# Block zero's v, r, q and k as seven half products, its weight pieces stored at once, a reordered end and one branch around two loops

## The chip, the cores and the metric

The kernel runs on one core of one Trainium2 chip. The metric is the device time of one launch in microseconds (us), the median of three runs.

## The reference, cut to what matters

A decoder block over 2048 tokens of width 1024. A projection makes q, k, v, r, a low-rank decay input, a pooling input u and two gates; the mixers' outputs are merged and projected; a router sends each token to two of 32 experts; a last norm ends it.

```python
h = rmsnorm(x, norm1_g)
q, k, v, r, a_low, u_pool, gate_gla, gate_pool = split(h @ w_in)
log_a = log_sigmoid(a_low @ w_alpha_up + b_alpha) / 16
o = head_rmsnorm(gla_mix(q, k, v, log_a), gla_norm_g) * silu(r)
y_gla  = o @ w_gla_branch
y_pool = pool_mix(u_pool, pool_w, pool_scale) @ w_pool_branch
x = x + (sigmoid(gate_gla) * y_gla + sigmoid(gate_pool) * y_pool) @ w_out
x = x + hier_moe(rmsnorm(x, norm2_g), ...)        # top-2 of 32 SwiGLU experts
return rmsnorm(x, norm_f_g)
```

## The kernel before

The mixer works on four blocks of 512 tokens (blocks 0 to 3, `block`, L802), the experts follow in 16 pairs (`moe`, L1131). Every projection is done in three passes of float16 halves: a float32 weight piece of 128x1024 is loaded on SyncE's queue (`stage`, L159), split into a high and a low half by one ScalarE instruction (L177) and one VectorE instruction (L178), and multiplied by the high and low halves of the activations. A split piece can be stored in HBM (L181, also on SyncE's queue) and only loaded in the later blocks (L170). `KEEP` (L193) says from which block on each kind of weight is stored: q, k, u (kind 0), v and r (kind 1), the output weight (kind 3) and the gla branch (kind 4) from block 1, gates and pool branch from block 0. So block 1 loads and splits again what block 0 has split. Float32 pieces and split pieces share one pool of 13 buffers (`NW`, L204).

Two projections that share their input (v with r, gate with gate, q with k, u with u) are done together in seven half-size products instead of eight, of weight pieces and differences of weight pieces (`less`, L395, on GpSimd, L398) with the activations `hT` and with sums and differences of the activations `hS` (`p0_norm`'s `sums`, L287; turned by DMA on SyncE's queue, `turn`, L261). The products are put together on VectorE (L348 for the 512 wide ones, L527 for those of q, k and u, 256 wide). `seven` (L323) takes the products in the order A11, S1, S3, S4, S2, A12, A22; S1 to S4 need `hS`, the A ones only `hT`.

Block 0 is different. Its v is done in whole products as soon as a token tile is turned (`p3v`, L594, called from `hybrid`, L1461), its r likewise (`p3r`, L600), and its q and k in whole products (`WHOLE`, L552, `whole` in `seven_c`, L508). The decay (`p1a`, `p1b`, `p1c`) stands between v and q.

At the end, each expert pair's three row groups are added up (`D`: L1322, L1334), normed, scaled and scattered to HBM (`F`: `finish`, L1339, `scatter`, L1283). Then come two loops over counts held in a table (`overflow`, L1374), which run zero times for these inputs. The order of instructions on each engine is set when the program is built, by a list scheduler.

Of the kernel before, what the change touches and what calls it, by code (L numbers as in the profile page):

```python
# [17 lines left out]
KT = 8  # L18
# [18 lines left out]
class Mixer:  # L37
# [51 lines left out]
    def consts2(self):  # L89
# [22 lines left out]
        self.g2q = self.cx.tile([128, D], F32, name="g2q")  # L112
        V.tensor_scalar(self.g2q, self.g2, float(D) ** 0.5, None, op0=OP.mult)
# [79 lines left out]
    KEEP = (1, 1, 0, 1, 1, 0)  # L193
# [22 lines left out]
    def normed(self, x, g, store=None, quick=False, new=None):  # L216

        nc = self.nc
        if quick:
# [11 lines left out]
            for y, n in zip(ys, q):  # L231
                nc.vector.scalar_tensor_tensor(y, x[:, n], r[:, 0:1], self.g2q[:, n], op0=OP.mult, op1=OP.mult)
# [319 lines left out]
    WHOLE = (1, 0)  # L552
# [54 lines left out]
    def p3(self, fill):  # L607
# [11 lines left out]
        self.seven(self.L7, V0, R0, self.et, post, fill)  # L619
# [182 lines left out]
    def block(self, b, tail):  # L802
# [60 lines left out]
        if last:  # L863
            self.xo = {t: self.x_load(b, t) for t in range(TT)}
# [206 lines left out]
    def spill(self):  # L1071
# [31 lines left out]
        V.tensor_scalar(none[:, 0:1], none[:, 0:1], 0.5, None, op0=OP.is_lt)  # L1103
        for _, _, l, _ in self.tab:
# [26 lines left out]
    def moe(self):  # L1131
# [18 lines left out]
        with tc.manual_schedule(engines={getattr(E, e) for e in self.MANUAL}) if self.MANUAL else ExitStack():  # L1150
            for P in range(self.NP + 1):
                for c in (self.PLAN if P else self.PLAN.replace("U0 A0 U1 A1", "V0 V1 W0 A0 W1 A1")).split():
# [186 lines left out]
    def finish(self, s, i):  # L1339

        nc = self.nc
        x, o, _, l, nl = s["X"][i]
        y, r = self.rstd(x)
# [7 lines left out]
        nc.vector.tensor_tensor(y, x, y, op=OP.mult)  # L1351
        t = self.scatter(y, o).ins
# [21 lines left out]
    def overflow(self):  # L1374
# [7 lines left out]
        with tc.For_i(0, n):  # L1382
            T = lambda name, sh, dt=F32: mp.tile([128] + sh, dt, name="o" + name)
            le = T("le", [32])
            V.tensor_scalar(le, self.ct, self.it, None, op0=OP.is_le)
            e = T("e", [1])
            V.tensor_reduce(e, le, axis=AX.X, op=OP.add)
            ei = T("ei", [1], I32)
            V.tensor_copy(ei, e)
            V.tensor_scalar(le, self.i32, e, None, op0=OP.is_equal)  # L1390
            st = T("st", [32])
            V.tensor_tensor(st, self.ct, self.nt, op=OP.subtract)
            V.tensor_tensor(st, st, le, op=OP.mult)
            base = T("base", [1])
            V.tensor_reduce(base, st, axis=AX.X, op=OP.add)
            V.tensor_tensor(base, self.it, base, op=OP.subtract)
            V.tensor_tensor(st, self.capE, le, op=OP.mult)
            cap = T("capt", [1])
            V.tensor_reduce(cap, st, axis=AX.X, op=OP.add)
            V.scalar_tensor_tensor(base, base, 128.0, cap, op0=OP.mult, op1=OP.add)  # L1400
            rel, oth = T("rel", [nt * 2]), T("oth", [nt * 2])
            V.tensor_scalar(oth, self.ex.rearrange("p t k -> p (t k)"), e, OOB, op0=OP.not_equal, op1=OP.mult)
            V.tensor_scalar(rel, self.rk.rearrange("p t k -> p (t k)"), base, None, op0=OP.subtract)
            V.tensor_tensor(rel, rel, oth, op=OP.add)
            io = T("io", [128])
            nc.gpsimd.iota(io, pattern=[[1, 128]], base=0, channel_multiplier=0, allow_small_or_imprecise_dtypes=True)
            pt = self.aux()
            for c in range(2 * nt):
                a = mp.tile([128, 128], F32, name="oA", bufs=1)
                V.tensor_scalar(a, io, rel[:, c:c + 1], None, op0=OP.is_equal)  # L1410
                nc.tensor.matmul(pt[:, 0:2], a, self.fld[:, c // 2, c % 2], start=c == 0, stop=c == 2 * nt - 1)
            tb = T("tb", [2, 1])
            V.tensor_copy(tb, pt[:, 0:2, None])
            ii, w, _, _ = self.columns(tb, "o", mp)
            er = nc.values_load(ei[0:1, 0:1], engines=[mybir.EngineType.SP], min_val=0, max_val=NE - 1,
# [32 lines left out]
def hybrid(tc, A, out, NTOK=2048, cap=CAP, dbg=None):  # L1448
    nc = tc.nc
    with ExitStack() as ctx:  # L1450
# [82 lines left out]
```

## Time and profile before

| | |
|---|---|
| time, median of 3 runs | 1668.42 us (1664.65 to 1674.61) |
| profiled execution: its own time | 1676.06 us |
| its span | 1674.3 us |
| mean granted TensorE clock | 0.96 |
| TensorE busy | 1530.3 us, 91% |
| VectorE busy | 1074.3 us, 64% |
| ScalarE / GpSimd busy | 686.0 us / 607.7 us |
| mean rate of the DMA engines | 236 GB/s |

A share is that of the whole span. The blocks lie at 0 to 336.5 us (block 0), to 627.7 us (block 1), to 898.4 us (block 2) and to about 1169 us (block 3); a block is counted from its first v or r matmul (in blocks 1 to 3, L339) to that of the next. The expert pairs follow.

### The profile page before, as it was taken

To read this page: it belongs to the slowest core of one execution; us is meant where nothing else is said; L and a number is where in the kernel's file an instruction comes from. 1 tells how busy PE (TensorE), PEld (TensorE's weight loads), DVE (VectorE), ACT (ScalarE), POOL (GpSimd) and SP (SyncE) were. 2 spreads that over 40 slices of the span, in tenths; PEclk is the share of its full clock that TensorE was granted. 3 is DMA by queue.
4 is the path that set the end of the run, shared out by engine and by line. 5 is a ranking of instruction groups with operands and counts; after the bars stand their busy time and mean duration, and the time that the engine had idled before them with its cause. 6 is when DMAs were issued, how large, how long until landed. Compare 5 with 4: busy or idle time off the path is not lost.

```text
span 1674.3 us, 27694 instructions
## 1 busy us (share of the span) xinstructions
PE 1530.3 (91%) x10587; PEld 914.6 (55%) x10587; DVE 1074.3 (64%) x1898; ACT 686.0 (41%) x1056; POOL 607.7 (36%) x543
## 2 busy tenths in 40 slices
PE   5898978987999898999989999996799999999994
PEld 3364333435744343764434674443668787777773
DVE  8669685589954543772624674337577777777762
ACT  5623453453223352122423021113356665666661
POOL 1356382356523401342322241121343444444431
PEclk9999999989999999999989999998799999999997
DMA  7434659797775989565878756759599999999941
GB/s 267 133 117 141 232 189 249 230 293 234 231 259 164 250 287 286 182 194 179 231 192 246 245 160 201 204 159 315 187 313 332 336 328 341 333 325 326 330 164 43
DMA packets 244808, 394.65 MB, mean 236 GB/s; under 512 B 154507, under 2 KB 157963, under 8 KB 244672
## 3 DMA queue, kind: packets, MB, share of 16 engines
q1 hardware_dynamic: 222144, 324.50, 62.5%
q0 software_dynamic: 22528, 68.35, 11.5%
q8 instruction: 84, 1.38, 0.3%
q14 instruction: 52, 0.43, 0.1%
HBM read 294.03 MB, written 75.50 MB: 221 GB/s over the span
## 4 chain that ended last, share of the span: by engine, by line
PE 66%; DVE 11%; DMA 7%; issue 6%; POOL 4%; SPq 3%; ACT 2%; POOLq 0%; DVEq 0%; ACTq 0%
PE acc L1297 14%; PE aux L339 8%; PE acc L774 8%; PE acc L339 8%; PE acc L1322 7%; PE acc L522 6%; PE acc L757 6%; DMA w<-in_wv_dram 4%; PE acc L1334 3%; DVE w L178 3%; DMA bt<-bt 2%; SPq L261 2%; PE auxh L1241 2%; PE acc L591 1%; POOL w L398 1%
## 5 line engine op out<-in xcount | busy, mean ns | idle before, releaser
L1297 PE MATMUL acc<-xT,mwh 128*128 128x184 f16 (+2 forms) x3264 | 249.8, 239 | 0.0
L1297 PEld LDWEIGHTS <-mwh 128*128 128x128 f16 x3264 | 244.6, 98 | 7.6 <-issue 7.6
L178 DVE SCALAR_TENSOR_TENSOR w<-w 128x1024 f16<-128x1024 f32 x106 | 144.2, 1369 | 88.5 <-ACT w L177 88.2
L774 PE MATMUL acc<-w,bt 128*128 128x512 f16 x768 | 174.4, 389 | 16.1 <-DMA bt<-bt 12.9
L339 PEld LDWEIGHTS <-hS 128*128 128x128 f16 x1056 | 104.5, 100 | 133.4 <-issue 18.0
L757 PE MATMUL acc<-w,bt 128*128 128x512 f16 x768 | 169.0, 381 | 7.1 <-ACT w L177 7.1
L177 ACT ACTIVATE w<-w 128x1024 f16<-128x1024 f32 x106 | 108.0, 1028 | 151.8 <-DMA w<-in_wv_dram 75.2
L1203 DVE SCALAR_TENSOR_TENSOR mwh<-mst,mwh 128x1024 f16<-128x1024 f32 x128 | 153.4, 1219 | 23.6 <-ACT mwh L1202 23.4
L1202 ACT ACTIVATE mwh<-mst 128x1024 f16<-128x1024 f32 x128 | 128.7, 1049 | 60.7 <-PE acc L1297 59.8
L774 PEld LDWEIGHTS <-bt 128*128 128x128 f16 x768 | 76.0, 100 | 113.2 <-issue 14.5
L339 PE MATMUL aux<-w,hS 128*128 128x512 f16 x528 | 131.6, 398 | 4.5 <-DVE w L178 2.5
L339 PEld LDWEIGHTS <-hT 128*128 128x128 f16 x792 | 77.2, 98 | 100.9 <-issue 11.1
L522 PEld LDWEIGHTS <-w 128*128 128x128 f16 x1176 | 114.3, 100 | 32.4 <-issue 10.5
L757 PEld LDWEIGHTS <-bt 128*128 128x128 f16 x768 | 75.3, 98 | 99.9 <-issue 10.9
L339 PE MATMUL acc<-w,hS 128*128 128x512 f16 x528 | 123.1, 382 | 0.0
L1322 PE MATMUL acc<-msd,sg 128*128 128x512 f32 x256 | 115.7, 605 | 0.0
L762 POOL TENSOR_TENSOR et<-et 128x512 f32<-128x512 f32 x32 | 40.5, 1269 | 174.9 <-DVE et L760 174.9
L684 ACT ACTIVATE bt<-et 128x512 f16<-128x512 f32 x48 | 30.2, 628 | 174.4 <-POOL et L762 100.6
L348 DVE SCALAR_TENSOR_TENSOR et<-aux,et 128x512 f32<-128x512 f32 x99 | 65.8, 683 | 53.5 <-PE aux L339 53.5
L339 PE MATMUL aux<-w,hT 128*128 128x512 f16 x396 | 91.8, 379 | 5.7 <-DVE w L178 3.3
L760 DVE SCALAR_TENSOR_TENSOR et<-acc,et 128x512 f32<-128x512 f32 x64 | 43.3, 689 | 82.4 <-PE acc L757 82.4
L339 PE MATMUL acc<-w,hT 128*128 128x512 f16 x396 | 92.3, 379 | 0.9 <-DVE w L178 0.9
(293 smaller groups left out, 2493.8 us busy)
## 6 DMA issues: line engine op xcount, KB each, us to landing
w<-wkeep SPq DMA_DIRECT2D x172, 512.0 KB, 4.7
mst<-in_we_dram SPq DMA_DIRECT2D x128, 512.0 KB, 6.0
wkeep<-w SPq DMA_DIRECT2D x70, 512.0 KB, 3.3
msd<-in_we_dram SPq DMA_DIRECT2D x64, 512.0 KB, 7.1
w<-in_wv_dram SPq DMA_DIRECT2D x60, 512.0 KB, 4.9
x<-in_x_dram SPq DMA_DIRECT2D x32, 512.0 KB, 5.5
w<-in_wm_dram SPq DMA_DIRECT2D x16, 512.0 KB, 6.1
out_dram<-x POOLq DMA_DIRECT2D x16, 512.0 KB, 5.8
```

The lines of the kernel that those rows point to most:

```text
L177: nc.scalar.activation(w[:, 0, c:], f[:, c:], AF.Copy, scale=WSC)
L178: nc.vector.scalar_tensor_tensor(w[:, 1, c:], f[:, c:], WSC, w[:, 0, c:], op0=OP.mult, op1=OP.subtract)
L339: nc.tensor.matmul(p, L[name](i, c, k), w[k // 2][:, a, (k % 2) * 512:(k % 2 + 1) * 512], start=k == 0 and m == 0, stop=k == 3 and m == 2)
L348: nc.vector.scalar_tensor_tensor(o[i], ps[i], DSC, x[i], op0=OP.mult, op1=OP.add)
L522: nc.tensor.matmul(ps[:, :h], w[:, i, k * 128:(k + 1) * 128], L[name](c, k), start=k == 0 and m == 0, stop=k == 3 and m == 2)
L757: nc.tensor.matmul(ps, lhs, w[k // 2][:, a, (k % 2) * 512:(k % 2 + 1) * 512], start=k == 0 and i == 0, stop=k == 3 and i == 2)
L774: nc.tensor.matmul(ps, self.mT[t][k // 4][:, 4 * c + k % 4], w[hf][k // 2][:, a, (k % 2) * 512:(k % 2 + 1) * 512], start=k == 0 and i == 0 ...
L1202: nc.scalar.activation(w[:, 0], f, AF.Copy, scale=WSC)
L1203: nc.vector.scalar_tensor_tensor(w[:, 1], f, WSC, w[:, 0], op0=OP.mult, op1=OP.subtract)
L1297: nc.tensor.matmul(ps[:, c * CAP + lo:c * CAP + hi], self.part(W[o], col, 128, a), xT[:, b, k, lo:hi], start=k == 0 and i == 0, stop=k == ...
L1322: nc.tensor.matmul(ps, s["ac"][i][:, f, :128], self.part(s["W"][3 * i + 2], f * D + hf * 512, 512), start=f == 0, stop=f == 1)
L1334: nc.tensor.matmul(ps[hf * 64:(hf + 1) * 64], s["ac"][h][:, f, CAP - 64:], self.part(s["W"][3 * h + 2], f * D + hf * 512, 512), start=q == ...
```

## The change

Block 0's v and r are done in seven half products too, as are its q and k (`WHOLE` is zero); all split pieces are stored from block 0 on (`KEEP` is zero). v and r get a product loop and a weight order of their own in every block, the two products that need no sums first. In block 0 all four tiles are normed and turned before the sums are formed, and the decay steps lie between the products. A scaled copy of the second norm's gain is dropped; the gain is scaled in place in block 3. The last two expert pairs norm by another sequence of instructions, the last pair does its third row group first, and one branch stands around both loops at the end (their bodies are unchanged, one level deeper).

```diff
-        self.g2q = self.cx.tile([128, D], F32, name="g2q")
-        V.tensor_scalar(self.g2q, self.g2, float(D) ** 0.5, None, op0=OP.mult)
...
-    KEEP = (1, 1, 0, 1, 1, 0)
+    KEEP = (0, 0, 0, 0, 0, 0)
...
-    def p0_turn(self, i, hh, dma=True):
-        if i == 0:
+    def p0_turn(self, i, hh, dma=True, parts=(0, 1)):
+        if i == 0 and 0 in parts:
...
-        for j, t in enumerate((i, i + 2)):
-            self.turn(hh[j], lambda a: H[:, a, :, t * 128:(t + 1) * 128], dma)
-        for j in range(2):
-            self.turn(hh[2 + j], lambda a: HS[:, i, j, a], True)
+        if 0 in parts:
+            for j, t in enumerate((i, i + 2)):
+                self.turn(hh[j], lambda a: H[:, a, :, t * 128:(t + 1) * 128], dma)
+        if 1 in parts:
+            for j in range(2):
+                self.turn(hh[2 + j], lambda a: HS[:, i, j, a], True)
...
-    WHOLE = (1, 0)
+    WHOLE = (0, 0)
...
-        self.seven(self.L7, V0, R0, self.et, post, fill)
+        self.seven_raw(self.L7, self.vr or self.pieces_raw(V0, R0), self.et, post, fill)
+        self.vr = None
...
+    def seven_raw(self, L, g, new, post, fill=()):
...
+        p = product("A11")
+        one = [new() for _ in I]
+        for i in I:
+            nc.scalar.activation(one[i], p[i], AF.Copy, scale=DSC)
+        c11 = add(product("A12"), one)
+        for i in I:
+            post(i, 0, c11[i])
+        c12 = add(product("S1"), one)
+        p = product("S3")
+        c22 = add(p, c12)
+        c21 = add(p, one, one)
+        p = product("S2")
+        for c in (c22, c12, c21):
+            add(p, c, c)
+        for i in I:
+            post(i + 2, 1, c22[i])
+        add(product("A22"), c21, c21)
+        for i in I:
+            post(i + 2, 0, c21[i])
+        add(product("S4"), c12, c12)
+        for i in I:
+            post(i, 1, c12[i])
+
+    def pieces_raw(self, n1, n2):
...
+        yield raw(b11)
+        yield raw(b21)
+        if first:
+            get(b12)
+        yield less(0, b11, b12, b11)
+        if first:
+            get(b22)
+        yield less(1, b12, b22, b12)
+        yield less(2, b11, b22, b11)
+        yield less(3, b21, b21, b11)
+        yield raw(b22, False)
...
+        self.v, self.rs = {}, {}
         if b:
-            self.v, self.rs = {}, {}
             self.p3([lambda: None] * self.N2 + tail[:4])
             tail[4]()
+        else:
+            self.p3([lambda: None] * 2 + [self.p1a, self.p1b, self.p1c])
...
-        if b == 0:
-            wr = [self.weight("wv", R0 + j) for j in range(4)]
-            self.p3r(0, wr)
-            self.p2t(1)
-            for t in range(1, TT):
-                self.p3r(t, wr)
-        else:
-            self.p2t(1)
+        self.p2t(1)
...
+            nc.vector.tensor_scalar(self.g2, self.g2, float(D) ** 0.5, None, op0=OP.mult)
...
+        self.gl = mp.tile([128, D], F32, name="gl")
+        nc.scalar.activation(self.gl, self.gf, AF.Identity, bias=self.lq[:, 1:2], scale=self.ln[:, 0:1])
...
+                if P == self.NP - 1:
+                    plan = plan.replace("D0 F0 D1 F1 D2 F2", "D2 F2 D0 F0 D1 F1")
...
     def finish(self, s, i):
...
+        if s["P"] >= 14:
...
+                for h in range(2):
+                    c = slice(h * 512, h * 512 + 512)
+                    nc.scalar.activation(y[:, c], x[:, c], AF.Square, accum_out=ss[:, h:h + 1])
+                nc.vector.tensor_scalar(r, ss[:, 0:1], ss[:, 1:2], D * EPS, op0=OP.add, op1=OP.add)
+                nc.gpsimd.tensor_tensor(r, r, self.mhalf[:, 0:1], op=OP.pow)
+                nc.vector.tensor_scalar(r, r, self.lq[:, 0:1], self.lq[:, 1:2], op0=OP.mult, op1=OP.add)
+                nc.vector.scalar_tensor_tensor(y, x, r, self.gl, op0=OP.mult, op1=OP.mult)
...
-        with tc.For_i(0, n):
...
+        with tc.If(n > 0):
+            with tc.For_i(0, n):
...
+            n = nc.values_load(self.tot[0:1, 1:2], min_val=0, max_val=nt, skip_runtime_bounds_check_because="0 or all tiles")
+            with tc.For_i(0, n) as t:
...
-        wv = [m.weight("wv", V0 + j) for j in range(4)]
-        m.v, m.rs = {}, {}
+        g = m.pieces_raw(V0, R0)
+        ws = [next(g) for _ in range(2)]
...
+        m.vr = both()
+        sums, hhs = [], []
         for i in range(2):
-            hh = []
-            for f in m.p0_norm(0, i, hh, nc.vector):
-                f()
-            m.p0_turn(i, hh, m.DM[0])
-            m.hT = m.hTn
-            for t in (i, i + 2):
-                m.p3v(t, wv)
+            hhs.append([])
+            n0, n1, s = m.p0_norm(0, i, hhs[i], nc.vector)
+            n0()
+            n1()
+            sums.append(s)
+            m.p0_turn(i, hhs[i], m.DM[0], (0,))
+        for i in range(2):
+            sums[i]()
+            m.p0_turn(i, hhs[i], m.DM[0], (1,))
         m.consts2()
-        m.p1a()
-        m.p1b()
-        m.p1c()
```

## Rows read from the trace of the kernel before

**Rows 1.** The profile's page: busy time of each engine, and the chain by engine.

```profile
PE 1530.3 (91%) x10587; PEld 914.6 (55%) x10587; DVE 1074.3 (64%) x1898; ACT 686.0 (41%) x1056; POOL 607.7 (36%) x543
...
PE 66%; DVE 11%; DMA 7%; issue 6%; POOL 4%; SPq 3%; ACT 2%; POOLq 0%; DVEq 0%; ACTq 0%
```

**Rows 2.** Busy time of each engine by stretch (us from the span's start).

```profile
core 0: us, PE busy (x) PEld busy (x) DVE busy (x) ACT busy (x) POOL busy (x), PEclk, DMA share, GB/s
0.00:138.00 138.00, 111.14 (x669) 65.21 (x670) 100.98 (x167) 71.22 (x109) 47.50 (x51) 0.95 0.51 162
138.00:288.00 150.00, 128.14 (x570) 55.64 (x568) 110.53 (x121) 65.88 (x98) 80.03 (x44) 0.97 0.68 209
...
336.50:460.50 124.00, 104.11 (x748) 67.94 (x747) 111.95 (x201) 49.77 (x90) 70.79 (x54) 0.92 0.80 253
460.50:627.70 167.20, 160.64 (x751) 72.07 (x749) 88.33 (x123) 61.96 (x92) 50.85 (x46) 0.98 0.82 240
627.70:730.30 102.60, 95.10 (x747) 65.45 (x746) 65.98 (x172) 19.42 (x54) 28.82 (x31) 0.97 0.75 217
730.30:898.40 168.10, 161.74 (x750) 72.47 (x748) 74.29 (x110) 53.10 (x84) 49.19 (x46) 0.97 0.71 204
```

**Rows 3.** The same view of L178, VectorE's split, alone.

```profile
336.50:460.50 124.00, 36.59 (x26) 0.92 0.80 253
460.50:627.70 167.20, 15.80 (x12) 0.98 0.82 240
```

**Rows 4.** The chain in order of time (start, us, what): two matmul runs.

```profile
90.14 12.52 PE acc L591 x58
...
448.16 3.60 PE acc L522 x32
```

**Rows 5.** VectorE's groups by shape: 0 to 60, then 60 to 336.5, then block 2.

```profile
L178 DVE SCALAR_TENSOR_TENSOR w<-w 128x1024 f16<-128x1024 f32 x11 | 13.4, 1221 | 9.2 <-ACT w L177 9.2
...
L178 DVE SCALAR_TENSOR_TENSOR w<-w 128x1024 f16<-128x1024 f32 x55 | 77.1, 1411 | 56.7 <-ACT w L177 56.7
...
L348 DVE SCALAR_TENSOR_TENSOR et<-aux,et 128x512 f32<-128x512 f32 x9 | 6.0, 684 | 3.3 <-PE aux L339 3.3
L527 DVE SCALAR_TENSOR_TENSOR bt<-acc,bt 128x256 f32<-128x256 f32 (+1 forms) x16 | 6.8, 453 | 4.6 <-PE acc L522 3.9 <-issue 0.7
```

**Rows 6.** GpSimd's groups by shape, 0 to 138 us.

```profile
L398 POOL TENSOR_TENSOR w<-w 128x1024 f32<-128x1024 f32 x4 | 9.4, 2354 | 19.0 <-DMA w<-in_wv_dram 19.0
...
L566 POOL TENSOR_TENSOR w<-w 128x512 f32<-128x512 f32 x2 | 3.0, 1500 | 0.0
```

**Rows 7.** Timelines of GpSimd and VectorE around 91 us (start, us, instruction).

```profile
91.15 1.29 POOL L569 TENSOR_TENSOR w<-w 128x512 f32<-128x512 f32 x1
...
91.11 2.42 DVE L178 SCALAR_TENSOR_TENSOR w<-w 128x1024 f16<-128x1024 f32 x1 [3.06 <-ACT w L177]
```

**Rows 8.** Timelines of SyncE's queue and of TensorE, the first 50 us.

```profile
28.75 5.42 SPq L261 DMA_TRANSPOSE hS<-et  x4
...
44.77 5.35 SPq L261 DMA_TRANSPOSE hS<-et  x4
...
18.27 3.58 PE L591 MATMUL acc<-w,hT 128*128 128x512 f16 x9
```

**Rows 9.** Block 0: DMA issues by line, and SyncE's longest waits (us, times, longest).

```profile
wkeep<-w SPq DMA_DIRECT2D x36, 512.0 KB, 3.0
...
SPq L181 <- DVE w L178: 81.1, 21, 9.2
```

**Rows 10.** The end: GpSimd's scatters, then instructions of three lines.

```profile
1657.18 1.03 POOL L1284 DMA_INDIRECT out_dram<-y,tim  x1 [1.37 <-DVE frs L1344]
1659.68 0.99 POOL L1284 DMA_INDIRECT out_dram<-y,tih  x1 [1.48 <-DVE y L1351]
...
L1438 SPq TENSOR_LOAD <-stot x1: 287/287/287, 1663.7 to 1663.7; - x1
...
L1439 POOLq COMPARE_BRANCH  x3: 33/33/39, 1665.2 to 1666.5; - x3
```

More of the change, by code (lines that the diff above doesn't have):

```diff
@@ L617, in post, with product, add @@
             self.rs[t] = x
-        self.seven(self.L7, V0, R0, self.et, post, fill)
+        self.seven_raw(self.L7, self.vr or self.pieces_raw(V0, R0), self.et, post, fill)
+        self.vr = None
+    vr = None
+    def seven_raw(self, L, g, new, post, fill=()):
+        nc = self.nc
+        I = range(2)
+        fill = list(fill)
+        def product(name):
+            if fill:
+                fill.pop(0)()
+            w, ps = next(g), []
+            for i in I:
+                p = self.acc() if i else self.aux()
+                for k in range(4):
+                    for m, (a, c) in enumerate(self.PASSES):
+                        nc.tensor.matmul(p, L[name](i, c, k), w[k // 2][:, a, (k % 2) * 512:(k % 2 + 1) * 512],
+                                         start=k == 0 and m == 0, stop=k == 3 and m == 2)
+                ps.append(p)
+            return ps
+        def add(ps, x, o=None):
+            o = o or [new() for _ in I]
+            for i in I:
+                nc.vector.scalar_tensor_tensor(o[i], ps[i], DSC, x[i], op0=OP.mult, op1=OP.add)
+            return o
+        p = product("A11")
[15 more added lines that the diff above has]
+        add(product("A22"), c21, c21)
+        for i in I:
+            post(i + 2, 0, c21[i])
+        add(product("S4"), c12, c12)
+        for i in I:
+            post(i, 1, c12[i])
@@ new lines, in pieces_raw, with raw, get, less @@
+    def pieces_raw(self, n1, n2):
+        I = range(2)
+        b11, b12, b21, b22 = ([n + 2 * k2 + j for j in I] for n, k2 in ((n1, 0), (n2, 0), (n1, 1), (n2, 1)))
+        first = (n1, 0) not in self.kept
+        T = {}
+        def raw(b, load=True):
+            if first and load:
+                get(b)
+            return [self.weight("wv", i, T.get(i)) for i in b]
+        def get(b):
+            for i in b:
+                T[i] = self.stage("wv", i)
+        def less(n, out, x, y):
+            if first:
+                for o, p, q in zip(out, x, y):
+                    self.on('less').tensor_tensor(T[o], T[p], T[q], op=OP.subtract)
+            return [self.weight(n1, 2 * n + j, T.get(out[j])) for j in I]
+        yield raw(b11)
[3 more added lines that the diff above has]
+        yield less(0, b11, b12, b11)
+        if first:
+            get(b22)
[3 more added lines that the diff above has]
+        yield raw(b22, False)
@@ L1151, in moe @@
             for P in range(self.NP + 1):
[L1152 removed]
+                plan = self.PLAN
+                if P == 0:
+                    plan = plan.replace("U0 A0 U1 A1", "V0 V1 W0 A0 W1 A1")
+                if P == self.NP - 1:
+                    plan = plan.replace("D0 F0 D1 F1 D2 F2", "D2 F2 D0 F0 D1 F1")
+                for c in plan.split():
                     f, d = {"U": (self.mo_up, 0), "V": (lambda s, h: self.mo_up(s, h, 0, 128), 0),
@@ L1381, in overflow @@
                            skip_runtime_bounds_check_because="counts of the rows bound it")
-        with tc.For_i(0, n):
[L1383 to L1415, printed above, removed]
-                                skip_runtime_bounds_check_because="a count of at most 31")
-            W = [[self.load(self.A["we"][bass.ds(er, 1), :, c:c + PW].rearrange("o p c -> p (o c)"), i == 2)
-                  for c in range(i * 2048, (i + 1) * 2048, PW)] for i in range(3)]
-            W = [[self.msplit(f, self.mw) for f in w] if i < 2 else w for i, w in enumerate(W)]
-            x = self.mxs[0]
-            o = self.out, ii
-            self.base1(x, o, True)
-            h = self.mhs[0]
-            self.gather(h, ii, True)
-            xT = mp.tile([128, 2, 2, KT, CAP], F16, name="xT", bufs=2)
-            for a in range(2):
-                pt = self.auxh()
-                for k in range(KT):
-                    nc.tensor.transpose(pt[:, k * 128:(k + 1) * 128], h[:, a * D + k * 128:a * D + (k + 1) * 128], self.identh)
-                self.evac(a, xT[:, 0, a, :, 0:128], pt.rearrange("p (k t) -> p k t", k=KT))
-            V.memset(xT[:, 0, :, :, 128:], 0.0)
-            s = {"W": W, "xT": xT, "ac": {}, "ps": {}}
-            self.mo_up(s, 0)
-            self.mo_act(s, 0)
-            self.mo_out(s, 0, x, w)
-            self.scatter(x, o)
-            V.tensor_scalar(self.it, self.it, 1.0, None, op0=OP.add)
```

95 lines of the change are left out of this document (85 added, 10 removed).

## The prediction

> **What bounds the kernel now.** I read the profile's page first [rows 1]. TensorE is busy for 91% of the span and holds 66% of the chain of waits, VectorE 11%, and SyncE's queue 3%. The kernel is bound by matmuls, with gaps. To find the gaps I cut the span by block [rows 2]. Blocks 1 and 2 run the same 1,500 or so matmuls. From its first v or r product to its first gate product block 1 takes 124.0 us and block 2 takes 102.6 us; from there to the end of the block they take 167.2 and 168.1 us. So block 1 is slower in its first part alone. There VectorE is busy 111.95 of 124.0 us (90%), against 65.98 of 102.6 in block 2, and TensorE idles 19.9 us at a granted clock of 0.92 against 7.5 us at 0.97. What VectorE does more is splitting: 26 splits in this part of block 1, 12 in its second part [rows 3], none in block 2, which has no piece left to split. The second part shows that splits cost nothing where VectorE has room: 12 of them, with their stores, and it is no longer than in block 2. In block 0, TensorE idles 26.9 us in the first 138 us and 21.9 us in the next 150 [rows 2], with VectorE busy 73% and 74%.
>
> **The change, part by part.**
>
> *Block 1 loses its splits and stores* (all kinds are stored from block 0 on). Its code is then that of block 2: it loads 74 stored pieces. I price it by block 2: 102.6 + 168.1 = 270.7 us in place of 124.0 + 167.2 = 291.2, so −20.5 us. Bounds: −15 if its start still waits for DMA turns behind block 0's tail, −25 if it gains something in its second part too (SyncE's queue no longer holds 12 stores there).
>
> *Block 0, TensorE.* v and r go from 192 matmuls of 512 columns to 168. A run of 58 takes 12.52 us, 0.216 us each [rows 4]: −5.2 us. q and k go from 96 of these (20.7 us) to 168 of 256 columns at 3.60/32 = 0.1125 us (18.9 us): −1.8 us. Together −7.0 us.
>
> *Block 0, VectorE before the gates.* v and r are 14 split pieces in place of 8, q and k 6 whole and 2 halves in place of 4. At 1.221 us for a split while GpSimd rests [rows 5], six are 7.3 us, and two with two halves 3.7 us. Putting together v and r takes 18 additions of 0.684 us, where four of that shape fall away: +9.6 us. Those of q and k take 6.8 us in block 2. Sum: +27.4 us, so 100.98 becomes 128.4 us of the 138 us before the gates [rows 2]. It fits, barely. ScalarE's ten more casts lie beside it; ScalarE is busy 71 of 138.
>
> *Block 0, GpSimd.* Eight differences of 2.354 us and, at 1.5 us, four products for r and eight half-piece differences for q and k [rows 6]: 18.8 + 18.0 = +36.8 us, so 47.5 becomes 84.3 of 138 us.
>
> *Block 0, order.* Today v needs only `hT`: 96 matmuls, 20.7 us of work, start at 18.27 us. The sums' turns are issued at 28.75 and at 44.77 us and end their issue at 50.1 [rows 8], and nobody misses them, since v, the decay, q, k and r need none. After the change only A11 and A12, 48 matmuls or 10.4 us, can run before the sums are there; then S1 wants both halves of `hS`. The sums are queued on VectorE behind four norms but no longer behind q's splits, so I estimate `hS` at about 40 us and TensorE idle for some 10 us before it, about what it idles there today; the decay's small matmuls can move into that gap.
>
> I take +3 us for block 0 as a whole. The lower bound is −7, matmuls gone and no new wait. For the upper bound: a split that lies under GpSimd's work takes 1.411 us on the mean instead of 1.221 [rows 5], 16% more. VectorE's 128.4 us, 15.5% longer, are 148.3 us, 10 beyond the present 138: +10. The value lies between, nearer the middle, since VectorE would be almost full and every late split is then a late matmul.
>
> The rule that speaks against this change: the Trainium skill's page "SBUF — State Buffer", section "SBUF: two separate sides", says that VectorE, in an instruction with two SBUF inputs, and GpSimd take one port pair in turns, each locked out for the other's whole instruction. One row agrees: a split at 91.11 us takes 2.42 us beside a GpSimd instruction of 1.29 us from 91.15 on [rows 7]; the mean, only 16% up, says that most escape. By the mean, block 0 ends at the +10 above; by the rule, it is the second rival.
>
> *42 stores move from block 1 to block 0.* Their bytes are the same. Block 0's part before the gates uses the DMA engines to 0.51, the next 150 us to 0.68, and block 1's second part lives at 0.82 without being slower than block 2 [rows 2]. So bandwidth costs nothing by these rows. But each store waits on SyncE's queue for its split, in order, and the loads and DMA turns issued after it wait too: that is the third rival.
>
> *The end.* With the third row group first, the pair's last scatter follows the second group. Its chain after the last matmul is shorter by one ScalarE instruction and the wait for a second norm: the next to last scatter is issued at 1657.18 today, the last at 1659.68 [rows 10]. I take −2.0 us, bounds 0 (that scatter moves twice as many bytes as the last one does now) and −2.5. The second loop takes 1663.7 to 1666.5 to find that it has nothing to do [rows 10]; the branch skips it, and first loop and branch are one check: −2.9 us, bounds 0, if the end waits for the scatter anyway, and −5.8, twice that.
>
> *At nothing:* the gain scaled in place (one VectorE instruction beside block 3's matmuls), the new ScalarE product for the last norm (at the experts' start ScalarE waits for gathers), and the other product order in blocks 1 to 3: same matmuls, same 18 additions, the sums turned a block ahead. If that cover is gone they cost under 1 us each, the order up to 3 us either way.
>
> **Sum.** −20.5 − 7.0 + 10.0 (waits, to the +3 above) − 2.0 − 2.9 = −22.4 us. Against the profiled execution: 1676.06 − 22.4 = 1653.7 us. The median of the three runs is 7.6 us below it; carried over, 1668.42 − 22.4 = 1646.0 us. A difference within 0.5% (8.3 us) is one that a measurement of this kernel hardly tells from none.
>
> **Rivals.** *More than that (chance 0.23).* Block 0 keeps its −7, the branch gives −5.8: −20.5 − 7 − 2 − 5.8 = −35.3, 1633 us. For it: VectorE's 27.4 us fit into its 37 idle us. Against it: its first idle stretches come before there is anything to split.
>
> *VectorE and GpSimd in turns: no change (0.11).* If every microsecond of GpSimd's 36.8 locked VectorE, 101.0 + 27.4 + 36.8 = 165.2 us would stand in place of 138: +27.2. Sum −20.5 + 27.2 − 4.9 = +1.8: 1670 us, block 1's gain given back in block 0. Against it: only splits and differences read two SBUF inputs; the additions read PSUM.
>
> *Stores block SyncE's queue: slower (0.06).* Block 0's 36 stores today wait 81.1 us in 21 waits, up to 9.2 us each [rows 9]; TensorE idles 21.9 us in the 150 us where most lie, 0.61 us a store. With 42 more the price is between 0 (hidden) and 3.9 us each (every wait a loss). The change is slower by over 8.3 us from 0.97 us a store on: −20.5 − 7 − 4.9 + 42 × 0.97 = 8.3. At twice today's rate, 1.22, it is +18.8, 1687 us. For it: 13 buffers hold up to eight float32 pieces in the new order, so a late store is a late load soon. Against it: block 1's 0 us for 12 stores.
>
> **How the numbers follow.** The forecast, 1646 us, gets 0.60, by itself 1637 to 1656. The range 1630 to 1662 takes in the better rival and all of the terms' bounds, −15 + 10 + 0 = −5 at the weak end cut by a little since they hardly meet; it leaves out both cases that give the gain back. Faster by over 0.5%: 0.60 + 0.23 = 0.83; within: 0.11; slower: 0.06.
>
> **What would show it.** In the new profile L178 runs 74 times, all in block 0, and all 74 stores too; block 1 lasts 266 to 276 us with VectorE under 75% in its first part; block 0 lasts 330 to 347 us, TensorE idling 5 to 15 us before the first product with `hS`; from the last scatter's issue to the span's end it is under 12.5 us, in place of 14.6 (1659.68 to 1674.3). The forecast is wrong if block 0 grows by over 15 us: then the splits' mean time (the second rival) or the waits of the store line on SyncE's queue (the third) say which.

## The result, and the profile after

The change made the kernel slower, by less than 1%: 1680.53 us (1677.35 to 1683.98) against 1668.42 for the kernel before, each the median of seven runs, where the table of the kernel before says three; the ratio is 1.0065, 95% interval 1.0048 to 1.0082. The forecast was 1646.

The profiled executions are nearer to each other than the medians: 1678.19 us (span 1676.3) against 1676.06. A single execution lies up to about 8 us from its kernel's median (before's is 7.6 above, the changed kernel's 2.3 below). So the stages below account for +2.1 us, and some 10 us of the difference between the medians can't be placed in a stage.

Rows of the changed kernel's page: TensorE, VectorE, and the loads and stores of split pieces.

```profile
PE 1523.5 (91%) x10635; PEld 917.0 (55%) x10635; DVE 1055.8 (63%) x1901; ACT 647.4 (39%) x1021; POOL 604.5 (36%) x539
...
w<-wkeep SPq DMA_DIRECT2D x210, 512.0 KB, 4.6
...
wkeep<-w SPq DMA_DIRECT2D x70, 512.0 KB, 3.3
```

The line of VectorE's split (now L176) and its duration: minimum, median, maximum in ns, then first and last start in us. All 74 lie in block 0, as foreseen; the last starts at 355 us, 15 us before the block's end.

```profile
L176 DVE SCALAR_TENSOR_TENSOR w<-w x74: 678/1220/3378, 17.3 to 355.1; 128x1024 f16<-128x1024 f32 x70, 128x512 f16<-128x512 f32 x4
```

Busy time by stretch. The first four rows are block 0: the head (up to the first gate product), the first gates, the second gates with the merges, the rest. Then blocks 1 and 2, each cut at its first gate product, as in [rows 2].

```profile
core 0: us, PE busy (x) PEld busy (x) DVE busy (x) ACT busy (x) POOL busy (x), PEclk, DMA share, GB/s
0.00:147.80 147.80, 110.95 (x716) 71.17 (x717) 130.32 (x195) 69.68 (x104) 81.53 (x65) 0.90 0.68 232
147.80:207.60 59.80, 44.36 (x178) 18.37 (x177) 49.55 (x62) 25.39 (x47) 37.70 (x21) 0.93 0.59 188
207.60:301.20 93.60, 68.02 (x275) 28.60 (x274) 62.06 (x61) 41.14 (x53) 50.16 (x28) 0.86 0.70 210
301.20:370.60 69.40, 67.01 (x316) 29.19 (x316) 32.98 (x37) 26.85 (x33) 15.42 (x14) 1.00 0.97 316
370.60:466.90 96.30, 93.85 (x747) 65.07 (x746) 69.30 (x177) 23.65 (x61) 30.03 (x32) 0.98 0.74 235
466.90:633.80 166.90, 160.25 (x751) 71.94 (x749) 74.39 (x110) 53.09 (x84) 49.19 (x46) 0.98 0.73 206
633.80:733.20 99.40, 93.73 (x748) 64.83 (x747) 66.05 (x168) 16.77 (x49) 28.14 (x29) 0.98 0.75 216
733.20:899.80 166.60, 160.50 (x751) 72.01 (x749) 74.35 (x110) 53.09 (x84) 49.14 (x46) 0.98 0.72 206
```

Block 1 did what was forecast and more: its first part fell from 124.0 to 96.3 us. It is block 0 that grew, from 336.6 to 370.6 us. Cut at the first matmul of each stage, its +34.0 us are: head +9.9, first gates +13.2, first merge +0.9, second gates +19.8, then −7.2 and −2.6 given back in the last two stages. Block 2 became 4.7 us shorter, block 3 and the experts 2.5 us longer, the end 2.1 us shorter.

TensorE over the whole of block 0, before and after, in the columns above:

```profile
0.00:336.60 336.60, 284.71 (x1433) 140.76 (x1434) 240.54 (x316) 158.74 (x231) 146.82 (x108) 0.96 0.62 195
...
0.00:370.60 370.60, 290.34 (x1480) 147.33 (x1481) 274.92 (x353) 163.05 (x236) 184.81 (x127) 0.91 0.72 235
```

TensorE is idle for 80.3 us of block 0 in place of 51.9, and busy for 5.6 us more though it has less to multiply; its mean granted clock there is 0.91 in place of 0.96.

**The head.** VectorE and GpSimd, then TensorE, timeline (start, us, instruction, idle before it and what ended it). GpSimd's lines are the eight differences of v and r.

```profile
28.25 2.00 DVE L154 SCALAR_TENSOR_TENSOR wrl<-w,wrh 128x288 f16<-128x288 f32 x1
30.17 2.84 DVE L289 TENSOR_TENSOR x<-x 128x512 f32<-128x512 f32 x1
...
34.13 3.36 DVE L176 SCALAR_TENSOR_TENSOR w<-w 128x1024 f16<-128x1024 f32 x1
...
50.69 3.37 DVE L251 TENSOR_TENSOR et<-x,et 128x1024 f16<-128x1024 f32 x1
...
26.64 5.81 POOL L691 TENSOR_TENSOR w<-w 128x1024 f32<-128x1024 f32 x2 [13.32 <-DMA w<-in_wv_dram]
33.93 2.48 POOL L691 TENSOR_TENSOR w<-w 128x1024 f32<-128x1024 f32 x1 [1.47 <-DMA w<-in_wv_dram]
37.58 5.47 POOL L691 TENSOR_TENSOR w<-w 128x1024 f32<-128x1024 f32 x2 [1.16 <-DVE w L176]
44.21 8.76 POOL L691 TENSOR_TENSOR w<-w 128x1024 f32<-128x1024 f32 x3 [1.16 <-DVE w L176]
...
46.32 0.61 PE L638 MATMUL aux<-w,hS 128*128 128x512 f16 x1 [11.19 <-DMA hS<-et]
...
53.34 2.08 PE L453 MATMUL aux<-bt,wau 128*128 128x512 f32 x2 [4.70 <-ACT et L652]
57.34 4.88 PE L638 MATMUL aux<-w,hS 128*128 128x512 f16 x11 [1.92 <-DMA hS<-et]
```

Between 28 and 54 us, eight VectorE instructions, one for each GpSimd difference, take longer than their kind does elsewhere, seven of them by some 2.1 us (a split 3.36 in place of 1.22, a sum 2.84 in place of 0.68), the first by 1.55: about 16.6 us in all. Only two are splits of weights for the products; three are sums. So `hS` comes late: TensorE waits 11.19 + 1.92 us for it, and 4.70 us for a ScalarE step of the decay in between, 17.8 us before the run of its products. The Trainium skill's page "SBUF — State Buffer", section "SBUF: two separate sides", says that such a VectorE instruction and a GpSimd instruction take the shared port pair in turns, each for its whole length; these rows agree as to the turns, one lengthened instruction for each difference; the 2.1 us are less than the 2.5 to 2.9 us that a difference takes in GpSimd's rows.

**The gates.** SyncE's queue, first the waits of the store line in block 0 (us, times, longest), then its timeline; last TensorE.

```profile
SPq L179 <- DVE w L176: 155.0, 45, 10.0
...
72.57 17.10 SPq L179 DMA_DIRECT2D wkeep<-w  x4
...
91.56 13.29 SPq L179 DMA_DIRECT2D wkeep<-w  x5
...
136.37 0.42 SPq L159 DMA_DIRECT2D w<-in_wv_dram  x1
...
257.24 18.16 SPq L179 DMA_DIRECT2D wkeep<-w  x4
275.49 0.38 SPq L159 DMA_DIRECT2D w<-in_wv_dram  x1
...
281.56 5.33 SPq L259 DMA_TRANSPOSE hT<-et  x4
286.98 5.36 SPq L259 DMA_TRANSPOSE hS<-et  x4
292.40 0.57 SPq L159 DMA_DIRECT2D w<-in_wv_dram  x1
...
296.92 3.78 PE L810 MATMUL aux<-w,pwt 128*128 128x512 f32 x4 [13.68 <-DMA w<-in_wv_dram]
```

TensorE's waits in the first gates (us, times, longest), and two of its runs behind the longest wait in the second:

```profile
PE aux L339 <- ACT w L175: 6.7, 2, 4.7
PE aux L339 <- DVE w L176: 4.5, 3, 2.3
...
270.69 1.86 PE L339 MATMUL aux<-w,hT 128*128 128x512 f16 x4 [4.89 <-DVE w L176]
...
275.11 1.02 PE L339 MATMUL aux<-w,hT 128*128 128x512 f16 x4 [0.85 <-DVE w L176]
```

The two places on SyncE's queue in the kernel before: the first gate load, and the pool branch's two loads.

```profile
97.37 1.76 SPq L161 DMA_DIRECT2D w<-in_wv_dram  x2
...
242.24 1.21 SPq L161 DMA_DIRECT2D w<-in_wv_dram  x2
```

The store line waits 155.0 us in 45 waits, against 81.1 in 21 [rows 9]. The first load for the gates is issued at 136.4 us in place of 97.4, 11 us ahead of the first gate product. So TensorE waits 11.2 us in the first gates for pieces to be split (before: 1.7). In the second gates the two pool-branch loads, once issued together, are 17 us apart: the first goes out behind four waiting stores, the second behind eight DMA turns for block 1, and TensorE waits 13.68 us for it. Behind such waits the matmuls are slower too: behind one of 4.89 us four of them take 1.86 us, soon after 1.02. Of the 33.0 us that the two gate stages grew by, 7.6 are TensorE's busy time, the rest its waits.

**The end.** GpSimd: the third group's scatter, the next group's norm behind it, the last scatter.

```profile
1660.10 1.76 POOL L1378 DMA_INDIRECT out_dram<-y,tih  x1 [2.64 <-ACTq L1501]
1661.89 0.58 POOL L1449 TENSOR_TENSOR frs<-frs,mhalf 128x1 f32<-128x1 f32 x1
...
1664.88 0.98 POOL L1378 DMA_INDIRECT out_dram<-y,tim  x1 [1.19 <-DVE y L1451]
```

From the last scatter's issue to the end of the span it is 11.4 us in place of 14.6, 3.2 saved; the branch alone, of what changed, stands there. From the last matmul (now over at 1657.05, before at 1652.90) to that scatter it is 7.8 us in place of 6.8.

### The profile page after: what moved, and what is told of

Its sections match the earlier page's. It is cut to its first block, busy times and chain, and to the rows that moved or that the text cites. A ratio compares the mean times of both kernels' runs of the same rounds, so it can differ in the third digit from the quotient of the medians.

```text
span 1676.3 us, 27617 instructions
## 1 busy us (share of the span) xinstructions
PE 1523.5 (91%) x10635; PEld 917.0 (55%) x10635; DVE 1055.8 (63%) x1901; ACT 647.4 (39%) x1021; POOL 604.5 (36%) x539
## 5 line engine op out<-in xcount | busy, mean ns | idle before, releaser
L1296 ACT ACTIVATE mwh<-mst 128x1024 f16<-128x1024 f32 x128 | 128.8, 1050 | 52.4 <-PE acc L1391 51.5
L522 PEld LDWEIGHTS <-w 128*128 128x128 f16 x1344 | 130.0, 99 | 26.6 <-issue 4.1
L176 DVE SCALAR_TENSOR_TENSOR w<-w 128x1024 f16<-128x1024 f32 x74 | 107.5, 1463 | 46.9 <-ACT w L175 46.8
L339 PEld LDWEIGHTS <-hS 128*128 128x128 f16 x768 | 75.9, 99 | 109.1 <-issue 21.4
L175 ACT ACTIVATE w<-w 128x1024 f16<-128x1024 f32 x74 | 74.9, 1029 | 99.7 <-DMA w<-in_wv_dram 37.4
L339 PE MATMUL aux<-w,hS 128*128 128x512 f16 x384 | 92.7, 385 | 14.4 <-ACT w L175 7.5
L339 PEld LDWEIGHTS <-hT 128*128 128x128 f16 x576 | 56.6, 98 | 78.3 <-issue 12.8
L522 PE MATMUL acc<-hS,w 128*128 128x256 f16 x768 | 94.7, 278 | 3.7 <-ACT w L175 2.0
L339 PE MATMUL acc<-w,hS 128*128 128x512 f16 x384 | 92.2, 384 | 0.0
L819 ACT ACTIVATE et<-et 128x512 f32<-128x512 f32 x64 | 39.7, 628 | 104.9 <-DVE et L348 104.7
L1416 PEld LDWEIGHTS acc<-msd,sg 128*128 128x128 f32 x256 | 48.0, 193 | 56.1 <-issue 47.0
```

What stands on the lines that cost most here:

```text
L175: nc.scalar.activation(w[:, 0, c:], f[:, c:], AF.Copy, scale=WSC)
L176: nc.vector.scalar_tensor_tensor(w[:, 1, c:], f[:, c:], WSC, w[:, 0, c:], op0=OP.mult, op1=OP.subtract)
L339: nc.tensor.matmul(p, L[name](i, c, k), w[k // 2][:, a, (k % 2) * 512:(k % 2 + 1) * 512], start=k == 0 and m == 0, stop=k == 3 and m == 2)
L522: nc.tensor.matmul(ps[:, :h], w[:, i, k * 128:(k + 1) * 128], L[name](c, k), start=k == 0 and m == 0, stop=k == 3 and m == 2)
L1296: nc.scalar.activation(w[:, 0], f, AF.Copy, scale=WSC)
L1416: nc.tensor.matmul(ps, s["ac"][i][:, f, :128], self.part(s["W"][3 * i + 2], f * D + hf * 512, 512), start=f == 0, stop=f == 1)
```

## The experiments

Two theories at the start. **S**: the added stores, waiting in order on SyncE's queue for their splits (or holding their buffers), make loads and turns late. **L**: VectorE's own added work in block 0, lengthened by GpSimd's lock, makes splits late. A table of all runs follows the edits; "storing kind n late" means from block 1 on.

**The kernel before again**, with no edit, for the scatter of a profile.

> The kernel before, profiled once more, nothing changed. The profiled execution on record was 7.6 us above the median of its runs. If that excess was in the blocks, block 0, 1 or 2 is shorter here than 336.5, 291.2 and 270.7 us, and the changed kernel's comparison by blocks shifts by as much; if it was elsewhere (experts, end), the blocks agree within 2 us.

Blocks 0, 1 and 2 took 338.4, 290.5 and 268.2 us (336.6, 290.9 and 270.7 in the first profile). In the run of the end alone, below, whose blocks are the same, they took 340.4, 293.3 and 265.6. So some 4 us of block 0 and 5 us of block 2 mean nothing in one profiled execution, and the 4.7 us of block 2 are within that.

**All kinds late**: the work of the change without its stores.

```diff
-    KEEP = (0, 0, 0, 0, 0, 0)
+    KEEP = (1, 1, 0, 1, 1, 0)
```

> The changed kernel with the old rule for storing (v, r, q, k, u, output and gla pieces from block 1 on): the 42 added stores leave block 0, block 1 splits again. Theory S (stores wait in order on SyncE's queue and make loads and turns behind them late): the gates and merges of block 0 take as long as in the kernel before, block 0 falls from 370.6 to about 345 us, block 1 is back at about 290, and the time is 1675 to 1685 us. Theory L (GpSimd and VectorE lock each other out, whatever the stores do): block 0 stays at 365 us or more, and the time is near 1705 us. Both expect the first gate product at about 148 us, since the start is not touched.

Block 0 took 361.2 us, between the two forecasts, and the ratio, 1.0240, came out a little above theory L's (1705 us is 1.022). The second gates were back at 51.8 us, but the head was 18 us over before's with no more stores in it (four, all of gate pieces). Both theories hold a part: without one added store block 0 is 24.6 us longer than before, and the 42 stores add 9.4 us to that. Block 1, which splits again, took 304.3 us in place of 290.9, nearly all of it in its first part (136.0 in place of 124.0); what makes it longer there than in the kernel before was not tried.

**Differences on VectorE**: the eight differences of v and r leave GpSimd.

```diff
-                    self.on('less').tensor_tensor(T[o], T[p], T[q], op=OP.subtract)
+                    self.nc.vector.tensor_tensor(T[o], T[p], T[q], op=OP.subtract)
```

> The changed kernel with the eight weight differences of v and r in block 0 on VectorE in place of GpSimd. Theory L: the eight waits of about 2.1 us (16.5 us in all between 28 and 54 us) go, eight instructions of 1.2 us (9.8 us) come, the turns of the sums are issued some 7 to 10 us earlier, TensorE's idle time between 33 and 57 us falls from 24 to about 15 us, the first gate product comes at 138 to 141 us, and the time falls by 6 to 10 us to 1671 to 1675 us. Theory S: the start gains no more than 3 us, because the sums' turns wait on SyncE's queue behind stores, or what it gains is lost again at the gates: 1678 to 1682 us.

VectorE's and TensorE's timeline, in the same stretch:

```profile
28.63 0.69 DVE L289 TENSOR_TENSOR x<-x 128x512 f32<-128x512 f32 x1
29.23 1.22 DVE L691 TENSOR_TENSOR w<-w 128x1024 f32<-128x1024 f32 x1
...
33.30 1.22 DVE L176 SCALAR_TENSOR_TENSOR w<-w 128x1024 f16<-128x1024 f32 x1
...
49.69 4.67 PE L638 MATMUL aux<-w,hS 128*128 128x512 f16 x11 [5.93 <-DMA hS<-et]
```

The lock is real: without GpSimd's differences VectorE's instructions in this stretch have their usual length, and the products with `hS` start 7.7 us earlier. But the gates start no earlier (148.7 us), and the ratio is that of the change: theory L's gain did not come.

**The end alone**, on the kernel before (`finish`, the pair's order, the branch).

```diff
+                if P == self.NP - 1:
+                    plan = plan.replace("D0 F0 D1 F1 D2 F2", "D2 F2 D0 F0 D1 F1")
...
+        with tc.If(n > 0):
```

> The kernel before with the changes at the end alone: the other norm of the last two pairs, the last pair's third row group first, one branch around both loops. The prediction's sum: 4.9 us faster (ratio 0.997). The trace of the changed kernel: from the last matmul to the end 19.3 us in place of 21.4, so 2.1 us faster (0.9987). Rival: the branch costs what it saves, no change.

0.9993 [0.9975, 1.0012]: the end is worth nothing that can be told here.

**One more buffer**; this and the next three are edits of the changed kernel.

```diff
-    NW, NET, NBT = 13, 19, 13
+    NW, NET, NBT = 14, 19, 13
```

> The changed kernel with 14 weight buffers in place of 13 (the dropped gain copy left the room). Theory S, in the form that the first runs leave: with 42 more stores holding buffers, SyncE's queue has the loads of block 0's second gate pass and of the pool branch behind late stores and behind eight turns; one more buffer puts loads earlier, the second gate pass falls from 72 to 55 to 65 us, block 0 to 353 to 364 us, and the ratio to the kernel before from 1.0065 to 0.996 to 1.002. Theory L (VectorE is full, in part because GpSimd locks it out): buffers change nothing, ratio 1.005 to 1.008, and the first gate product stays at 148 us.

Second gates 73.6 us, as without it: the buffer form of S fails there, and the ratio is as theory L had it, though the first gate product came at 144.4 us and not at 148.

**Stores on ScalarE's queue.**

```diff
-    KQ = 'sync'
+    KQ = 'scalar'
```

> The changed kernel with the stores issued from ScalarE's queue in place of SyncE's. Theory S: the loads and turns no longer stand behind stores that wait for splits; block 0 falls by 10 to 20 us to 350 to 360 us, ratio 0.995 to 1.001, less what ScalarE loses by waiting itself. Theory L: ScalarE now waits for VectorE's splits, its casts come later, block 0 is 370 us or longer, ratio 1.006 or more.

The second gates fell to 57.8 us, but the first rose to 65.2, and block 0 stayed at 369.9. S is right on the second gates alone; L has block 0, and the ratio lies between the two.

**Output weight and gla branch (kinds 3, 4) late.**

```diff
-    KEEP = (0, 0, 0, 0, 0, 0)
+    KEEP = (0, 0, 0, 1, 1, 0)
```

> The changed kernel with the output and gla pieces stored from block 1 on, as before: 12 of the 42 added stores leave the last third of block 0, and block 1 splits 12 pieces in its second part. Theory S: the pool-branch piece is loaded before the turns again, the second gate pass falls from 72 to 52 to 58 us, block 0 to 350 to 357 us, block 1's second part stays at about 168 us (as in the kernel before), ratio 0.995 to 0.999. Theory L: block 0 unchanged within 5 us, ratio 1.005 to 1.008.

Second gates 52.1 us, as S had it, though block 0 (362.5 us) and the ratio gained less than it forecast. SyncE's queue and TensorE there: the pool branch's loads go out as a pair again, ahead of the turns, and TensorE waits 2.00 us.

```profile
254.25 12.54 SPq L179 DMA_DIRECT2D wkeep<-w  x4
266.88 1.23 SPq L159 DMA_DIRECT2D w<-in_wv_dram  x2
...
278.79 5.55 SPq L259 DMA_TRANSPOSE hS<-et  x4
...
271.81 3.36 PE L810 MATMUL aux<-w,pwt 128*128 128x512 f32 x4 [2.00 <-DMA w<-in_wv_dram]
```

**q and k whole, with q, k, u late.**

```diff
-    WHOLE = (0, 0)
+    WHOLE = (1, 0)
-    KEEP = (0, 0, 0, 0, 0, 0)
+    KEEP = (1, 0, 0, 0, 0, 0)
```

> The changed kernel with q and k of block 0 in whole products as before, and q, k and u stored from block 1 on. Theory L: VectorE has about 10 us less to do before the gates and GpSimd about 12, so the first gate product comes at 138 to 142 us in place of 148 though TensorE has 1.8 us more to do; block 1 splits 16 pieces again and is some 10 us longer; ratio 1.003 to 1.008. Theory S: the start gains only what 16 fewer stores give, under 4 us, and the ratio is 1.010 or more.

First gates 50.6 us, second gates 75.7, block 1 at 283.4. The first gate product still came at 148.9 us: theory L fails here, and S has both the start and the ratio.

**The q and k part and the end**, on the kernel before.

```diff
-    KEEP = (1, 1, 0, 1, 1, 0)
+    KEEP = (0, 1, 0, 1, 1, 0)
-    WHOLE = (1, 0)
+    WHOLE = (0, 0)
```

> Before with two parts of the change: q and k of block 0 in seven products with the pieces of q, k and u stored from block 0 on, and the new end. v and r of block 0 stay whole products, so r's 96 matmuls still stand between q, k and the gates, and v, r, output weight and gla branch are stored from block 1 on as before. Theory H (block 0's loss is v and r in seven products, with VectorE full ahead of the gates and r's matmuls gone as cover): block 0 within 5 us of 336 to 340, block 1 loses 12 of 26 splits of its first part, about 10 us, to some 281; with the end's 2 to 3 us the ratio is 0.992 to 0.995. Theory S (any store added ahead of block 0's gates holds back the gates' loads on SyncE's queue, whatever stands before them): block 0 +8 us or more, ratio 0.997 to 1.001.

Theory H falls: r's whole products were there as cover, and the head still grew by 12 us. Block 1 became 15 us shorter, block 0 9 to 11 longer, and the timed ratio is 1.0017 (its profiled execution, 6.6 us under its median, shows better than that). Block 0 grew as S had it, but the first gates took no longer than before, so that it was the gates' loads is not shown.

**The same with 14 buffers** (and without the scaled copy of the gain).

```diff
-        self.g2q = self.cx.tile([128, D], F32, name="g2q")
...
-    NW, NET, NBT = 13, 19, 13
+    NW, NET, NBT = 14, 19, 13
```

> As the q and k part with the new end, and also the scaled copy of the gain dropped as the change does, its room used for a 14th weight buffer. The run of the changed kernel with 14 buffers gained nothing (1.0052 against 1.0065). If buffers still don't matter where fewer pieces are live: within 0.15% of the kernel without the 14th buffer. If they set when the gates' loads start: block 0 4 us or more shorter, 0.25% faster.

No gain: block 0 is 3.1 us longer than without the buffer and the ratio is 1.0036, a little more than the first forecast allowed.

**The changed kernel with q, k, u alone late.**

```diff
-    KEEP = (0, 0, 0, 0, 0, 0)
+    KEEP = (1, 0, 0, 0, 0, 0)
```

> The changed kernel with q, k and u alone stored from block 1 on (12 splits and 12 stores go back to block 1; q and k of block 0 are still done in seven products). It tells what lengthens block 0's gates before their merge from 46.6 to 59.8 us. Theory S (the 12 stores hold back the gates' loads): the stretch falls to 50 to 52 us, as in the run with q and k whole, block 0 to some 362, block 1 back up to 278 to 284, ratio 1.007 to 1.010. Theory L (VectorE's work for q and k in seven products, split, put together and locked out by GpSimd): the stretch stays at 58 to 62 us, block 0 at 368 to 372, block 1 278 to 284, ratio 1.011 to 1.015.

First gates 53.9 us, nearer to S, but the head took 151.4 and block 0 became only 1.9 us shorter, while block 1 became 23.3 us longer, more than both theories gave it; the ratio is above both ranges. Storing these 12 pieces in block 0 is worth 1.2% in the changed kernel.

**Three together**: differences on VectorE, 14 buffers, kinds 3 and 4 late.

```diff
-                    self.on('less').tensor_tensor(T[o], T[p], T[q], op=OP.subtract)
+                    self.nc.vector.tensor_tensor(T[o], T[p], T[q], op=OP.subtract)
...
-    NW, NET, NBT = 13, 19, 13
+    NW, NET, NBT = 14, 19, 13
-    KEEP = (0, 0, 0, 0, 0, 0)
+    KEEP = (0, 0, 0, 1, 1, 0)
```

> The changed kernel with three edits that were tried alone: the eight v and r differences of block 0 on VectorE (alone 1.0071), 14 buffers (alone 1.0052), output weight and gla branch stored from block 1 on (alone 1.0013). If they only add up, the third alone counts: 1.000 to 1.003. If the first two were hidden by the stores' waits behind them, and show once 12 stores are gone: block 0 at 352 to 358 in place of 362.5, ratio 0.995 to 0.998.

0.9948 [0.9932, 0.9964]: faster than the kernel before, and so than the changed one. Block 0 is back to 348.7 us with block 1 at 266.8, a little past the second forecast: the three don't add up, they need each other.

**Without the 14th buffer**, and **without the differences on VectorE**: each of the last kernel's first two edits undone in turn (`NW` at 13; `on('less')` again).

> The kernel of the three edits with 13 buffers again: differences on VectorE, output weight and gla branch stored from block 1 on. Theory L (GpSimd's eight differences lock VectorE in the head; with them gone the gates' loads can be issued earlier): ratio 0.994 to 0.997, block 0 348 to 353. Theory B (the 14th buffer lets the gates' loads run ahead, which the run with 14 buffers alone could not show behind 12 more stores): ratio 1.000 to 1.002, block 0 358 to 363.

> The kernel of the three edits with the eight differences on GpSimd again: 14 buffers, output weight and gla branch stored from block 1 on. Theory L: ratio 1.000 to 1.002, block 0 358 to 363, the head's VectorE instructions at 2.8 to 3.4 us again. Theory B: ratio 0.994 to 0.997, block 0 348 to 353. If the two only work together: both runs near 1.000.

1.0025 and 0.9994, block 0 at 359.2 and 359.4: neither theory as stated, the two work only together. TensorE's waits from 140 to 210 us (us, times, longest), first three together, then without the 14th buffer:

```profile
PE aux L339 <- ACT et L354: 5.8, 1, 5.8
PE aux L810 <- DMA w<-in_wv_dram: 1.3, 1, 1.3
...
PE aux L731 <- DVE sT L725: 0.4, 1, 0.4
```

```profile
PE aux L339 <- ACT et L354: 6.2, 1, 6.2
PE aux L810 <- DMA w<-in_wv_dram: 5.5, 1, 5.5
PE aux L731 <- DVE sT L725: 4.0, 1, 4.0
```

With the buffer TensorE waits 4.2 us less for a pool-branch load, and 3.6 us less for VectorE ahead of the gates.

**The v and r part**: three together, with q and k whole and q, k, u late.

```diff
-    WHOLE = (0, 0)
+    WHOLE = (1, 0)
-    KEEP = (0, 0, 0, 1, 1, 0)
+    KEEP = (1, 0, 0, 1, 1, 0)
```

> The v and r part by itself, with the new end and without the lock: v and r of block 0 in seven products, their differences on VectorE, 14 buffers, v and r stored from block 0 on; q and k of block 0 whole, and q, k, u, output weight and gla branch stored from block 1 on as before. Block 1 loses 14 of 26 splits of its first part, 11.5 us of its 21.4 by their share. Theory H (v and r in seven products lengthen block 0 by some 12 us whatever stands around them, as q and k did by 9): block 0 at 348 to 352, block 1 at 277 to 282, ratio 0.998 to 1.001. If v and r cost block 0 nothing once the lock is gone: block 0 at 336 to 342, ratio 0.992 to 0.995.

Block 0 at 349.7, 11 us over that of the kernel before run again, and block 1 at 282.2, both near theory H; the ratio, 1.0032, is above its range.

All runs (us, one profiled execution each; head is up to the first gate product; first and second gates are from a gates' first product to the first merge matmul after it). A ratio stands against runs of the kernel before made with it.

| kernel | head | first gates | second gates | block 0 | block 1 | ratio [95%] |
|---|---|---|---|---|---|---|
| before | 137.9 | 46.6 | 52.2 | 336.6 | 290.9 | 1 |
| before again | 137.6 | 46.8 | 54.0 | 338.4 | 290.5 | 1 |
| changed | 147.8 | 59.8 | 72.0 | 370.6 | 263.2 | 1.0065 [1.0048, 1.0082] |
| all late | 156.3 | 52.4 | 51.8 | 361.2 | 304.3 | 1.0240 [1.0203, 1.0277] |
| differences on VectorE | 148.7 | 56.0 | 72.7 | 368.4 | 263.7 | 1.0071 [1.0047, 1.0094] |
| end alone | 138.2 | 46.4 | 55.4 | 340.4 | 293.3 | 0.9993 [0.9975, 1.0012] |
| 14 buffers | 144.4 | 59.7 | 73.6 | 369.5 | 265.7 | 1.0052 [1.0032, 1.0072] |
| ScalarE's queue | 147.2 | 65.2 | 57.8 | 369.9 | 268.3 | 1.0052 [1.0031, 1.0073] |
| kinds 3, 4 late | 148.9 | 59.9 | 52.1 | 362.5 | 269.6 | 1.0013 [1.0001, 1.0025] |
| q, k whole, q, k, u late | 148.9 | 50.6 | 75.7 | 365.9 | 283.4 | 1.0119 [1.0096, 1.0143] |
| q, k part | 149.5 | 44.7 | 52.0 | 347.2 | 275.9 | 1.0017 [1.0003, 1.0031] |
| q, k part, 14 buffers | 147.9 | 48.4 | 54.2 | 350.3 | 280.7 | 1.0036 [1.0020, 1.0053] |
| q, k, u late | 151.4 | 53.9 | 72.8 | 368.7 | 286.5 | 1.0187 [1.0161, 1.0214] |
| three together | 144.2 | 50.8 | 53.8 | 348.7 | 266.8 | 0.9948 [0.9932, 0.9964] |
| … 13 buffers | 147.3 | 56.4 | 55.0 | 359.2 | 270.7 | 1.0025 [1.0015, 1.0036] |
| … GpSimd's differences | 147.8 | 58.2 | 52.3 | 359.4 | 266.2 | 0.9994 [0.9980, 1.0009] |
| v, r part | 142.2 | 54.4 | 55.4 | 349.7 | 282.2 | 1.0032 [1.0016, 1.0048] |

One column sorts itself: the second gates take 72 to 76 us in all five kernels that store kinds 3 and 4 in block 0 on SyncE's queue, and 52 to 58 in the rest. In each of the five TensorE waits 13.6 to 15.8 us there for the second pool-branch load, issued behind eight turns.

## Why the prediction was wrong

- *Block 1 loses its splits: −20.5 us.* Right, and under-sized: −27.7. Its first part, at 96.3 us, beats even block 2 of before. That splits cost nothing in its second part held within a few us: with 12 of them and their stores back there, block 1 was 6.4 us longer (263.2 to 269.6).
- *Block 0 as a whole: +3 us, bounds −7 to +10.* **This step failed**: +34.0. It was added up from −7.0 for matmuls and +10.0 for waits. The waits rose by 28.4 us, and TensorE's busy time by 5.6: the −7.0 was priced at matmuls of full speed, and part of them ran slower behind the waits (0.91 in place of 0.96 over the block; the same block was busy 284.71 and 289.54 us in the two profiles of the kernel before). The bound of +10 was worked out for the head alone. The head did come out at it, +9.9, with VectorE at 130.32 us of work (forecast 128.4) and GpSimd at 81.53 (84.3), but by luck: the bound supposed VectorE full for 148 us, and it was idle for 17.5 of the head's 147.8. What was left out is what is late next. The two gate stages took +13.2 and +19.8 us more: the gates' first load went out at 136 us and not at 97, and the second pool-branch load stood behind stores and turns. The extra work by itself makes most of it, +24.6 us with no store added; the stores make +9.4.
- *hS at about 40 us, some 10 us idle.* Too good: the real run of products with `hS` began at 57.3 us after 17.8 us of waits, 13.1 of them for `hS`.
- *The port lock, second rival, +27.2.* Its mechanism was there, some 16.6 us of VectorE's time in the head, and two readings had hidden it. The 1.411 us are the mean of all 55 splits from 60 us on, not of those beside GpSimd's work (62 splits after the change: 1.452). And not only splits and differences read two SBUF inputs: the lock fell on three sums and on steps of the norm too, which TensorE needed next. But taking it away alone gained nothing; with kinds 3 and 4 late and a 14th buffer it did (0.9994 with the lock, 0.9948 without).
- *42 stores cost nothing in bandwidth.* No row speaks against it: block 0's last two stages, at a DMA share of 0.97, were 9.8 us shorter than before. Their price was their place. *The third rival, stores block SyncE's queue,* had the sign and much of the mechanism, with a chance of 0.06. The two signs that the prediction named point at it: the splits' mean rose from 1.411 to 1.452 us only, the store line's waits from 81.1 to 155.0. But those waits are no measure of the loss, most of which came without the stores. Storing kinds 3 and 4 in block 0 costs 0.5% (1.0065 against 1.0013), shown by undoing it. It isn't a price for each store, though: the 12 of q, k and u gain 1.2% there.
- *The end: −2.0 and −2.9.* The branch gave 3.2. The new order gave nothing (+1.0): the last group's norm on GpSimd stood behind the third group's 1.76 us scatter. Together they are within a measurement's noise.
- *At nothing: the new order in later blocks.* Block 2 shows no more than the scatter of a profile; block 3 with the experts took 2.5 us longer. In a block that splits it is not nothing as far as the run with all kinds late shows, +12 us in block 1's first part, but there it may be something else that the scheduler moved.

Against the profiled execution, 1653.7 forecast and 1678.19 measured: block 0 +31.0, block 1 −7.2, block 2 −4.7, block 3 and experts +2.5, end +2.8, 24.4 us in all.

Open: what the extra work holds up in block 0 to make it 24.6 us longer, and why parts that gain nothing alone gain together. q and k in seven products (1.0017) and v and r in seven products (1.0032), each with its stores, are no faster than the kernel before, and on the changed kernel neither the 14th buffer (1.0052) nor the differences on VectorE (1.0071) gains; with kinds 3 and 4 late, all of these at once are 0.5% faster than the kernel before. A list scheduler orders every engine's instructions anew for each edit, so no run isolates a step without moving others. Nor was it tried to issue only the late pool-branch load earlier.

## What to carry to other kernels

Work that moves into a stage must be priced in the stages behind it too: ask which prefetch the filled engine and queue now delay, and bound that wait, not the filled stretch alone. On SyncE's queue here a store that waited for its split held up the loads behind it (18.16 us for one group of four), so look at a store's place as well as at its bytes. When several resources are nearly full at once, undoing one suspected cost can show little: try the undoings together, and then take them back one by one.

## What the runs showed of the hardware

Eight GpSimd subtractions of two float32 128x1024 tiles, 2.5 to 2.9 us each, each lengthened one VectorE instruction with two SBUF inputs, seven of them by some 2.1 us (0.68 to 2.84, 1.22 to 3.36), one by 1.55 (0.45 to 2.00); the same eight subtractions on VectorE take 1.22 us each. In this stretch moving them to VectorE costs it 9.8 us and frees it of 16.6.
